# Turning the probabilities of an attention layer by DMA instead of on TensorE

## The chip, the cores and the metric

The kernel runs on one core of a Trainium2 chip. Times are microseconds (us) of device time of one execution of the whole program.

## The reference

A two-layer streaming encoder, one inference step. There are 2048 prompt tokens (one sequence) and 64 sample tokens with caches of earlier keys and values; the model width is 1024. Both layers do

```python
q, k, v, gate = project(x, norm_g, w_in, q_g, k_g, n_heads, n_kv)   # RMS norm, one projection, RMS norm of q and k by head
o = attend(q, k, v, bias, valid, sinks)                              # softmax(q k / 8 + bias) v in a band of chunks of 64
y = x + (o * silu(gate)) @ w_out
```

Layer A has 16 query heads and 2 key heads, a band of the own chunk and 2 before it, and sinks. Layer B has 16 heads of 64 with keys and values of their own, a band of the own chunk and 8 before it, and a learned bias by clipped distance. For a tile of 128 query tokens of layer B the band is 640 keys wide, five blocks of 128. The results are the new activations of prompt and sample and the rolled key and value caches.

## The kernel before

The program is one long stream for TensorE, written out by hand in order; the other engines are ordered by a scheduler, which follows the order of the program text where it sees no reason against it. All DMAs are issued from the queue of SP (`load` and `store` are both `nc.sync.dma_start`), which works strictly in order: an instruction that waits holds up all behind it.

Two things are interleaved on TensorE. The `Filler` runs through jobs of projections (input projections of the layer, then the output projection), and the attention of the layer runs beside it: `pipeline()` in `layer_b` emits a piece of attention, calls `filler.to(mark)` to put in projection matmuls up to a mark, emits the next piece, and so on. Small work of the other engines (norms of q and k, splits of weights, copies) waits in a `Background` queue and is handed out by budget (`bg.share`).

Precision comes from splitting: a number is kept as a high and a low half, and a product is the sum of two or three matmuls. In layer B the weights (`wh`, `wl`), the activations (`xx`), the values (`VH`, both halves side by side in 128 columns) and the probabilities (`ph`, `pl`) are f16 halves; q and k are fp32r halves.

Layer B works by head pair (8 of them) and unit (8 units of 256 prompt tokens, two tiles each, and one unit of 64 sample tokens). A prompt unit has four steps, one for each tile `i` and head `h`, in the order (0,0), (1,0), (0,1), (1,1). One step:

- `scores(it, i, h)`: matmuls of q (L1354) and of its low half (L1355) against the band's keys into a PSUM buffer "sb"; DVE adds the bias and takes the minimum (L1358); ACT takes the exponential of up to 640 columns and its sum (L1362). `p` now holds the probabilities with queries on partitions, in a buffer of three.
- filler matmuls, half a step of them;
- `values` of the step before: up to five turns on TensorE (`transpose`, a helper, so all have line L799) bring `p` into another "sb" buffer with keys on partitions; ACT copies it to the high half `ph`, scaled (L774), DVE computes the low half `pl` (L775);
- `products` of a head, when both of its tiles are done: 12 matmuls of values against `ph` and `pl` (L1449). The short ones, for blocks that only one tile has, stand between the turns of `values`; the others follow.
- filler matmuls, the other half of the step.

After the second head, `finish_pairs` adds the halves, multiplies by the gate and stores to `ogb` (L1196 to L1200), from where the output projection loads it.

The queries and keys of the next unit are prepared in `queries`, after the second step of a unit. It copies the high half of q to the other partitions by two DMAs (L1301). Activations are loaded again for each head pair from a DRAM copy (`xsb`), one chunk of 256 KB in each of `XN = 7` buffers (L501); raw weights go through `WB = 3` buffers (L430). A new head pair's weights are prepared under the running one's units; `scan` loads of later weights measure their range.

Of the kernel before, what the change touches and what calls it, by code (L numbers as in the profile page):

```python
# [19 lines left out]
KC = 8  # L20
# [30 lines left out]
HB, WB_, PB, VB = 2.0 ** 10, 2.0 ** 14, 2.0 ** 14, 16.0  # L51

@with_exitstack
def hybrid_encoder_kernel(
# [152 lines left out]
    def input_across(h):  # L207
        across(h, h + 1)
        e, r, o = row[:, 16:17], row[:, 17:18], row[:, 20:23]
        powers(row[:, h : h + 1], e, r)  # L210
        times(o[:, 0:1], r, WB_)
        times(o[:, 1:2], e, 1 / (HB * WB_))
        times(o[:, 2:3], e, 0.5 / (VB * PB))
# [197 lines left out]
    def load_weights(g, *specs, scale=None):  # L411
# [75 lines left out]
    def load_act(  # L487
# [9 lines left out]

        if cached:
# [14 lines left out]
        def split(c):  # L513
            def fn():
# [3 lines left out]
                xx = t("xx", [P, 4 * OT], XN, dt)  # L518
# [19 lines left out]
                if cache is not None:  # L538
                    store(kept(c), wide(xx[:, : 4 * T]))
                if not squares:  # L540
                    fetch()
# [227 lines left out]
    def split_to(dst_hi, dst_lo, src, scale=None):  # L769
# [8 lines left out]
        return a, b  # L778

# [411 lines left out]
    def finish_pairs(Ov, gtv, n, dst):  # L1191
# [8 lines left out]
        store(dst, o1v)  # L1200


    def layer_b():
# [4 lines left out]
        def add_unit(hp, unit):  # L1208
# [21 lines left out]
            def gen():  # L1230
# [3 lines left out]
                if "VH" not in held:  # L1234
                    held["VH"] = t("values", [P, NT, 2, P], 1, F16)
# [37 lines left out]
        def queries(it):  # L1273
# [25 lines left out]
            if it not in its[-2:]:  # L1299
# [21 lines left out]
        def scores(it, i, h):  # L1321
# [5 lines left out]
            if i == 0 and h == 0:  # L1327
# [5 lines left out]
                it.base = 0 if u == NU else max(tt - 4, 0)  # L1333
# [23 lines left out]
            for r, b, c in soft:  # L1357
# [3 lines left out]
                )  # L1361
            ex = nc.scalar.activation(  # L1362
# [3 lines left out]
            bg.anchor(mi, ex)  # L1366
            if c == w - 1:
# [15 lines left out]
        def values(it, i, h, short):  # L1383
            u, T, tiles = it.unit
            tt, t0, n = tiles[i]
            if i == 0:
                it.ph[h], it.pl[h] = (
                    t(x, [P, 5, 256], 2, F32R if u == NU else F16) for x in ("ph", "pl")
                )
            if u == NU:  # L1390
                n, m, kb = P, 3, 0
            else:
                kt0 = max(tt - 4, 0)
                m, kb = tt - kt0 + 1, kt0 - it.base
            PT = psum_b("sb", 1024, 2)
            PTv = PT.rearrange("p (c x) -> p c x", x=P)
            for c in range(m):
                transpose(PTv[:, (kb + c) % 5, :n], it.p[i, h][:n, c * P : (c + 1) * P])
                if short:
                    short.pop(0)()  # L1400
            while short:
                short.pop(0)()
            bg.anchor(*split_to(
                it.ph[h][:, :m, t0 : t0 + n], it.pl[h][:, :m, t0 : t0 + n], PTv[:, :m, :n],
                None if u == NU else PB,
            ))

        def then(it, i, h):
            if it.unit[0] == NU:
                return [([], lambda: sample_outputs(it)), ([], lambda: sample_turned(it))]  # L1410
            if i == len(it.unit[2]) - 1:
                return [products(it, h)]
            return []
# [23 lines left out]
        def products(it, h):  # L1437
            u, T, tiles = it.unit
            ta, tb = tiles[0][0], tiles[1][0]
            VH = held["VH"]  # L1440
            full = [(VH[:, kt, h], kt - it.base, 0, UT) for kt in range(max(tb - 4, 0), ta + 1)]
            short = [(VH[:, ta - 4, h], ta - 4 - it.base, 0, P)] if ta >= 4 else []
            short.append((VH[:, tb, h], (tb - it.base) % 5, P, UT))
            last = len(full) - 1

            def product(x, low, start=False, stop=False):
                vt, c, q0, q1_ = x
                p = (it.ph, it.pl)[low][h]
                nc.tensor.matmul(it.O[:, h * T + q0 : h * T + q1_], vt, p[:, c, q0:q1_], start=start, stop=stop)  # L1449
# [312 lines left out]
```

## Time and profile before

| | us |
|---|---|
| median of 3 runs | 2256.91 |
| lowest and highest | 2255.82, 2259.93 |
| the profiled execution | 2247.8 |
| its span, first to last instruction | 2245.8 |

The profile is one execution. Layer A and its output projection take up to about 900 us, the attention of layer B runs from about 950 to 2100 us, and the output projection of layer B ends the program. The rows of a group give the line, the engine, the operation and the tiles, then the busy time and the mean duration of one in nanoseconds, then the time that the engine stood idle just before them and what ended it. A row of the timeline gives start, duration, engine, line and tile. "SPq" is the queue of SP, with the time that it takes to issue a DMA.

### The profile page before, as it was taken

The numbers are of one execution on the slowest core, as the hardware profiler recorded it, in microseconds if no ns is written. First come the engines' busy times: TensorE is split into PE (matmuls) and PEld (weight loads), VectorE is DVE, ScalarE is ACT, GpSimd is POOL, SyncE is SP. The second block draws the span as 40 slices with busy tenths as digits, with TensorE's granted clock in tenths as the row PEclk, the third lists the DMA queues.
The fourth block names the chain that finished last, engine by engine and source line by source line (L and its number), as shares of the span: only waits on it lengthen the run. The fifth ranks groups of instructions, "written<-read, shape, count | busy, mean of one in ns | idle before, by whom it ended". The sixth has DMA issues, their size and how long they took to land.

```text
span 2245.8 us, 42218 instructions
## 1 busy us (share of the span) xinstructions
PE 2175.2 (97%) x13931; PEld 1650.5 (73%) x13931; DVE 1565.0 (70%) x4042; ACT 1422.5 (63%) x3610; POOL 858.9 (38%) x1396
## 2 busy tenths in 40 slices
PE   7999999999999998989999999999999999999999
PEld 6888888888889996556666666666666666567888
DVE  6769777677675556777777776777777777677543
ACT  6878777777784333676666666766666667566421
POOL 5645544343454455753333233332333333232000
PEclk9999999999999999999999999999999999999999
DMA  8856547856446666444243333443443424233664
GB/s 272 281 166 218 179 138 223 240 176 193 162 139 193 222 192 213 149 134 138 87 151 112 117 119 108 131 122 96 123 124 108 133 87 133 82 92 121 186 201 156
DMA packets 274811, 349.00 MB, mean 155 GB/s; under 512 B 32080, under 2 KB 195680, under 8 KB 274560
## 3 DMA queue, kind: packets, MB, share of 16 engines
q1 hardware_dynamic: 274592, 346.30, 50.0%
q8 instruction: 110, 1.80, 0.3%
q14 instruction: 109, 0.89, 0.1%
HBM read 257.59 MB, written 73.43 MB: 147 GB/s over the span
## 4 chain that ended last, share of the span: by engine, by line
PE 37%; DVE 9%; ACT 6%; DMA 4%; issue 3%; POOL 1%; SPq 0%; ACTq 0%; DVEq 0%; POOLq 0%
PE pj L640 6%; PE pj L642 6%; PE pj L641 6%; PE sb L799 4%; PE o L1449 3%; DVE pl L775 2%; PE pj L1605 2%; PE pj L1607 2%; PE pj L1606 2%; DMA scan<-in_w_in_b_dram 2%; ACT p L1362 2%; DVE p L1358 2%; PE sb L1354 2%; PE sb L1355 2%; DMA scan<-in_w_o_b_dram 1%
## 5 line engine op out<-in xcount | busy, mean ns | idle before, releaser
L640 PE MATMUL pj<-wh,xx 128*128 128x512 f16 (+2 forms) x1648 | 639.9, 388 | 2.9 <-ACT pb L663 1.5
L641 PE MATMUL pj<-wl,xx 128*128 128x512 f16 (+2 forms) x1648 | 624.6, 379 | 5.5 <-DVE wl L451 5.5
L642 PE MATMUL pj<-wh,xx 128*128 128x512 f16 (+2 forms) x1648 | 624.7, 379 | 1.3 <-POOL xx L530 1.3
L1362 ACT ACTIVATE p<-p,nm 128x640 f32<-128x640 f32 (+5 forms) x264 | 199.4, 755 | 238.4 <-DVE nm L1358 236.0
L1605 PE MATMUL pj<-xx,wh 128*128 128x264 f32 (+1 forms) x1024 | 289.5, 283 | 3.0 <-DVE res L1615 1.3
L1607 PE MATMUL pj<-xx,wl 128*128 128x264 f32 (+1 forms) x1024 | 286.4, 280 | 1.7 <-DVE wl L441 1.1
L1606 PE MATMUL pj<-xx,wh 128*128 128x264 f32 (+1 forms) x1024 | 287.0, 280 | 0.0
L775 DVE SCALAR_TENSOR_TENSOR pl<-sb,ph 128x640 f16<-128x640 f32 (+4 forms) x256 | 188.9, 738 | 107.4 <-ACT ph L774 104.6
L799 PE MATMUL sb<-ident,p 128*128 128x128 f32 x1144 | 205.9, 277 | 14.2 <-DVE pl L775 12.6
L530 POOL TENSOR_TENSOR xx<-xraw,xx 128x528 fp32r<-128x528 f32 (+4 forms) x144 | 182.7, 1288 | 93.6 <-ACT xx L529 84.2
L1199 POOL TENSOR_TENSOR o<-gt,o 128x256 f32<-128x256 f32 (+1 forms) x132 | 100.0, 757 | 309.4 <-ACT p L1107 89.4
L1358 DVE CUSTOM_DVE_ANT_0 p<-sb,BT 128x640 f32<-128x640 f32 (+5 forms) x272 | 196.2, 721 | 26.3 <-PE sb L1355 22.0
L799 PEld LDWEIGHTS sb<-ident,p 128*128 128x128 f32 x1144 | 148.2, 141 | 72.0 <-DVE pl L775 25.1
L722 POOL TENSOR_TENSOR f<-f,mhalf 128x4 f32<-128x4 f32 (+2 forms) x187 | 192.8, 1031 | 14.4
L717 POOL TENSOR_TENSOR sq<-pa 128x256 f32<-128x256 f32 (+2 forms) x187 | 113.3, 606 | 214.3 <-ACT pa L676 145.9
L642 PEld LDWEIGHTS <-xx 128*128 128x128 f16 x1024 | 100.7, 98 | 126.5 <-issue 5.2
L774 ACT ACTIVATE ph<-sb 128x640 f16<-128x640 f32 (+4 forms) x256 | 160.4, 627 | 50.7 <-PE sb L799 49.3
L1107 ACT ACTIVATE p<-p,nm 128x257 f32<-128x257 f32 (+2 forms) x272 | 134.3, 497 | 45.5 <-DVE nm L1101 40.5
L640 PEld LDWEIGHTS <-xx 128*128 128x128 f16 x1024 | 100.4, 98 | 78.4 <-issue 2.2
L641 PEld LDWEIGHTS <-xx 128*128 128x128 f16 x1024 | 101.1, 99 | 67.5 <-issue 2.1
L1449 PE MATMUL o<-pl,values 128*128 128x256 f16 (+1 forms) x672 | 148.9, 255 | 0.0
L1449 PEld LDWEIGHTS <-values 128*128 128x128 f16 x1344 | 133.3, 100 | 16.0
(255 smaller groups left out, 5100.1 us busy)
## 6 DMA issues: line engine op xcount, KB each, us to landing
xx<-xsb SPq DMA_DIRECT2D x224, 256.0 KB, 2.8
xx<-xsa SPq DMA_DIRECT2D x88, 512.0 KB, 4.8
xraw<-oga SPq DMA_DIRECT2D x64, 264.0 KB, 3.6
xraw<-ogb SPq DMA_DIRECT2D x64, 264.0 KB, 3.3
xsa<-xx SPq DMA_DIRECT2D x32, 512.0 KB, 4.1
scan<-in_w_in_b_dram SPq DMA_DIRECT2D x64, 256.0 KB, 3.5
wraw<-in_w_in_b_dram SPq DMA_DIRECT2D x64, 256.0 KB, 3.3
q<-q SPq DMA_DIRECT2D x250, 64.0 KB, 2.3
```

The source lines that it names most:

```text
L640: nc.tensor.matmul(ps[:n, :C], xh, wh, start=k == 0, stop=False)
L641: nc.tensor.matmul(ps[:n, :C], xh, wl, start=False, stop=False)
L642: nc.tensor.matmul(ps[:n, :C], xl, wh, start=False, stop=k == KC - 1)
L722: nc.gpsimd.tensor_tensor(fv, fv, mhalf[:n, :H], op=ALU.pow)
L775: b = nc.vector.scalar_tensor_tensor(dst_lo, src, scale, wide(dst_hi), op0=ALU.mult, op1=ALU.subtract)
L799: nc.tensor.transpose(out, in_, ident[:n, :n])
L1358: mi = nc.vector.tensor_tensor_reduce(out=p[r, :nk], in0=S[r, o : o + nk], in1=b, op0=ALU.add, op1=ALU.min, scale=1.0, scalar=3e38, accum_ ...
L1362: ex = nc.scalar.activation(p[:n, :nk], p[:n, :nk], AF.Exp, scale=-1.0, bias=it.nm[:n, c : c + 1], accum_out=it.sm[:n, c : c + 1],)
L1449: nc.tensor.matmul(it.O[:, h * T + q0 : h * T + q1_], vt, p[:, c, q0:q1_], start=start, stop=stop)
L1605: nc.tensor.matmul(ps[:, :OT], wh, oh, start=k == 0, stop=False)
L1606: nc.tensor.matmul(ps[:, :OT], wh, ol, start=False, stop=False)
L1607: nc.tensor.matmul(ps[:, :OT], wl, oh, start=False, stop=k == KC - 1)
```

## The change

Layer B no longer turns its prompt probabilities on TensorE. After the exponential, ACT copies `p` to f16 (the high half) and GpSimd subtracts it from `p` (the low half), both into one of three buffers `two`, half and half by block, cut out of memory that the values do not use. The factor 2^14 that the scaled copy had applied is put into the exponent (an addition of its logarithm on DVE ahead of the exponential). One step later `turn_p` issues a transposing DMA that turns all blocks and halves of the step, up to 128 x 1280 f16, into `ph` (first head) or `pl` (second head). The products of a head follow three steps (`LAG`) after the scores of its second tile, in one burst; `moving` picks the block, for both tiles at once by a strided access where both have it. The sample unit keeps its turns on TensorE.

Beside that: two activation chunks share a buffer slot of layer B, so that its loads and the stores of the cached copy move two chunks at once; scaled raw weights go into the twelve buffers "wl", and both halves of a weight block into one "wh" buffer; and the stores of outputs, keys and values and the copies of q are kept in a list `held["later"]` and issued at the next `flush()`, half a step later. The turn of the gate uses an "sb" buffer in place of "tp".

```diff
+LAG = 3
+HALF = 5 * 2 * P
@@ fetch and split of load_weights
-                if spare and c % 2 and c > WB:
+                if scale is not None:
+                    raw = t("wl", [P, 512], WN)
+                elif spare and c % 2 and c > WB:
...
-                w.h = wh = t("wh", [P, J, C], WN, dt)
-                w.l = wl = t("wl", [P, J, C], WN, dt)
+                if scale is None:
+                    wh, wl = (t(x, [P, J, C], WN, dt) for x in ("wh", "wl"))
+                else:
+                    both = t("wh", [P, 2, C], WN, dt)
+                    wh, wl = both[:, 0:1], both[:, 1:2]
+                w.h, w.l = wh, wl
@@ load_act
+        if cached and dt == F16:
+            for c in (0, 2):
+                xx = t("xx", [P, 8 * OT], XN, dt)
+                held["last"] = load(
+                    xx[:, : 8 * T], cache[:, o * 2 * KC + 4 * c * T : o * 2 * KC + 4 * (c + 2) * T]
+                ).ins
+                x.parts += [parts_of(xx[:, 4 * T * e : 4 * T * (e + 1)], T, joint) for e in range(2)]
+            return x
@@ store_kv
-            store(kdst, ko[rows])
-            store(vdst, v)
+            if layer:
+                held["later"].append(lambda: (store(kdst, ko[rows]), store(vdst, v)))
...
@@ queries
+            def copies():
                 for hh, rows in enumerate(halves):
                     load(q1[hh][halves[1 - hh]].bitcast(F32), q1[hh][rows].bitcast(F32))
+
+            if it not in its[-2:]:
+                held["later"].append(copies)
@@ scores
+            if u != NU:
+                nc.vector.tensor_scalar(
+                    it.nm[:, c : c + 1], it.nm[:, c : c + 1], math.log(PB), 1.0,
+                    op0=ALU.add, op1=ALU.mult,
+                )
             ex = nc.scalar.activation(
...
+            if u != NU:
+                parts(it, i, h, p, nk // P)
...
+        def parts(it, i, h, p, m):
+            held["turn"] = r = (held["turn"] + 1) % 3
+            it.two = it.two if i or h else {}
+            it.two[i, h] = two = held["two"][:, 5 * r : 5 * r + m]
+            pv = p.rearrange("p (c q) -> p c q", q=P)[:, :m]
+            hi = nc.scalar.copy(two[:, :, 0, :], pv)
+            lo = nc.gpsimd.tensor_tensor(two[:, :, 1, :], pv, two[:, :, 0, :], op=ALU.subtract)
+            bg.anchor(hi, lo)
+
+        def turn_p(it, i, h):
+            if i == 0:
+                it.ph[h] = t(("ph", "pl")[h], [P, 2 * HALF], 2, F16)
+            two = it.two[i, h].rearrange("p c l q -> p (c l q)")
+            m = two.shape[1]
+            nc.sync.dma_start_transpose(
+                it.ph[h][:, HALF * i : HALF * i + m].rearrange("p (c q) -> p c q", q=P), two
+            )
...
+            todo = [(1, lambda: turn_p(it, i, h))]
             if i == len(it.unit[2]) - 1:
-                return [products(it, h)]
-            return []
+                todo.append((LAG, lambda: products(it, h)))
+            return todo
@@ products
+            for kt in [kb] + [k for k in range(ka, tb + 1) if k != kb]:
+                for low in range(2):
+                    x, q0, q1_ = moving(kt, low)
+                    nc.tensor.matmul(
+                        it.O[:, h * T + q0 : h * T + q1_], held["VH"][:, kt, h], x,
+                        start=kt == kb and not low, stop=kt == tb and low == 1,
+                    )
...
+        def flush():
+            later, held["later"] = held["later"], []
+            for fn in later:
+                fn()
@@ pipeline, in each step
+            def due(at):
+                flush()
+                now = [fn for d, fn in todo if d <= at]
+                todo[:] = [(d, fn) for d, fn in todo if d > at]
+                for fn in now:
+                    fn()
...
                     scores(it, i, h)
                     bg.share(BL, BP_, KC)
                     goal(2 * y + 1)
-                    short, nxt = todo.pop(0) if todo else ([], None)
-                    if prev is not None:
-                        values(*prev, short)
-                        bg.share(BL, BP_, KC)
-                        todo += then(*prev)
...
+                    due(step)
+                    bg.share(BL, BP_, KC)
+                    todo += [(step + d, fn) for d, fn in then(it, i, h)]
+                    step += 1
```

More of the change, by code (lines that the diff above doesn't have):

```diff
@@ L1199, in finish_pairs @@
         nc.gpsimd.tensor_tensor(o1v, gtv, o1v, op=ALU.mult)
-        store(dst, o1v)
+        if later:
+            held["later"].append(lambda: store(dst, o1v))
+        else:
+            store(dst, o1v)
     def layer_b():
@@ L1396, in values @@
             PTv = PT.rearrange("p (c x) -> p c x", x=P)
[L1397 to L1406, printed above, removed]
+            for c in range(3):
+                transpose(PTv[:, c, :], it.p[0, 0][:, c * P : (c + 1) * P])
@@ L1439, in products @@
             ta, tb = tiles[0][0], tiles[1][0]
[L1440 to L1449, printed above, removed]
@@ L1525, in pipeline @@
                 assert x + 2 >= len(its) or its[x + 2].ready
[L1526 to L1527 removed]
             while todo:
                 filler.to(filler.done + 2.6)
[L1530 to L1533 removed]
+                due(step)
+                step += 1
+            due(step)
         return pipeline
```

121 lines of the change are left out of this document (65 added, 56 removed).

## The prediction

> **What bounds the kernel now.** I read the page's head first, then the windows of layer B, then the groups by line, and last the timeline of one unit, engine by engine.
>
> ```profile
> span 2245.8 us, 42218 instructions
> PE 2175.2 (97%) x13931; PEld 1650.5 (73%) x13931; DVE 1565.0 (70%) x4042; ACT 1422.5 (63%) x3610; POOL 858.9 (38%) x1396
> 1200.00:1400.00 200.00, 197.42 (x1230) 129.44 (x1228) 145.70 (x374) 127.54 (x332) 65.00 (x119) 1.00 0.38 113
> L799 PE MATMUL sb<-ident,p 128*128 128x128 f32 x1144 | 205.9, 277 | 14.2 <-DVE pl L775 12.6
> ```
>
> PE (TensorE) bounds it: it is busy for 97% of the span and for 197.4 of 200 us in the middle of layer B, at full clock, while in the same stretch DVE has 145.7, ACT 127.5, POOL 65.0 and the DMA engines a share of 0.38 at 113 GB/s. The group that the change attacks is the last row: PE turns the probabilities block by block, 1144 times. Of these, 3 in each of 8 head pairs belong to the sample unit and stay, so 1120 go. But the 205.9 us are not what their removal is worth: matmuls overlap, and what counts is how far apart they start.
>
> ```profile
> 1402.66 0.28 PE L799 MATMUL sb<-ident,p 128*128 128x128 f32 x1
> 1402.77 0.22 PE L1449 MATMUL o<-pl,values 128*128 128x128 f16 x1
> 1402.83 0.28 PE L799 MATMUL sb<-ident,p 128*128 128x128 f32 x1
> 1408.84 0.71 PE L799 MATMUL sb<-ident,p 128*128 128x128 f32 x5
> 1409.38 0.38 PE L640 MATMUL pj<-wh,xx 128*128 128x512 f16 x1
> 1415.34 0.52 PE L1354 MATMUL sb<-KA,q 128*128 128x384 f32 x1
> 1432.71 0.53 PE L1354 MATMUL sb<-KA,q 128*128 128x384 f32 x1
> ```
>
> Five turns start at 1408.84 and the next projection matmul at 1409.38: 0.54 us, 0.108 us each. Where a product stands between two turns, the turn is again 0.11 us of the 0.17 (1402.66 to 1402.77). The last two rows are the first scores of two consecutive units (two token tiles, two heads, so four steps): 17.37 us per unit, 4.34 per step. The 1120 turns make 56 full units of 20.
>
> **What goes from PE.** 1120 turns at 0.109 us: -122.1 us. With them goes the wait for the PSUM buffer in which they land (12.6 us, the releaser "DVE pl L775" of the row above). The products stay: as many matmuls on the same columns, only gathered in one burst, since their place between turns hid nothing (a short product costs its 0.06 us there too). A full unit becomes 17.37 - 20 x 0.109 = 15.2 us, a step 3.8.
>
> **What the other engines get.** All of it must fit in 15.2 us per unit; 200 us of the window hold 11.5 units.
>
> ```profile
> L774 ACT ACTIVATE ph<-sb 128x640 f16<-128x640 f32 x192 | 133.0, 693 | 37.7 <-PE sb L799 36.8
> L775 DVE SCALAR_TENSOR_TENSOR pl<-sb,ph 128x640 f16<-128x640 f32 x192 | 157.7, 822 | 87.1 <-ACT ph L774 84.8
> L1358 DVE DVE_READ_ACCUMULATOR2_ANT nm<- 128x1 f32 x256 | 21.1, 82 | 0.0
> L530 POOL TENSOR_TENSOR xx<-xraw,xx 128x528 fp32r<-128x528 f32 x64 | 88.3, 1408 | 63.8 <-ACT xx L529 57.1 <-issue 6.6
> L530 POOL TENSOR_TENSOR xx<-xraw,xx 128x512 f16<-128x512 f32 x32 | 37.9, 1203 | 8.7 <-ACT xx L529 6.1 <-DMA xraw<-x 2.6
> L529 ACT CAST xx<-xraw 128x528 fp32r<-128x528 f32 x64 | 39.6, 633 | 31.3 <-PE pj L1607 28.4
> ```
>
> ACT: the high half was a scaled copy out of PSUM (0.69 us), and is now a copy out of SBUF; by the 128x528 cast, 0.633 x 640/528 = 0.77. ACT goes from 127.5/11.5 = 11.1 to 11.4 us. DVE loses 0.82 and gets a 128x1 addition (about the 0.08 of the accumulator read) per step: 12.7 to 9.7. POOL gets the subtraction that DVE had: 1.203 x 640/512 = 1.50 by the nearer row (f16 out), 1.408 x 640/528 = 1.71 by the other; I take 1.6, so 5.65 + 6.4 = 12.1 of 15.2. POOL is the next engine, at 79%, but under PE. To pass PE the subtraction would have to take 2.4 us.
>
> **The transfers.** 256 transposing DMAs of 128x1280 f16 (327,680 bytes in a full step) are new, 144 plain ones go (activation chunks in pairs). No row shows a transposing transfer. What rows show:
>
> ```profile
> q<-q SPq DMA_DIRECT2D x250, 64.0 KB, 2.3
> xx<-xsb SPq DMA_DIRECT2D x224, 256.0 KB, 2.8
> 1417.77 0.38 SPq L501 DMA_DIRECT2D xx<-xsb  x1
> 1407.09 0.32 SPq L1200 DMA_DIRECT2D ogb<-o  x1
> 1434.93 0.42 SPq L783 DMA_DIRECT2D res<-in_ckt_b_dram  x1
> ```
>
> An issue holds SP's queue for 0.32 to 0.42 us whatever its size, and 256 KB land after 2.8. The lower bound of a transpose is that: 0.38 us of the queue, 3.0 to landing. The upper bound takes it as ten transfers of one 128x128 block each: 3.8 us of the queue. (Landing one pair of blocks after another like the 64 KB row would be 5 x 2.3 = 11.5 us; that is a rival below.) In the built program 9.65 plain issues stand beside each four transposes, 3.7 us. So SP holds 5.2 us per unit at the lower bound and 18.9 at the upper; the transposes must stay under (15.2 - 3.7)/4 = 2.9 us of the queue not to bound the kernel, and at 3.4 the gain is gone. I take the lower half, since each is one instruction and the nearest rows do not grow with size. Data: 4 x 327,680 bytes at 113/0.38 = 297 GB/s are 4.4 us beside the 6.6 there are: 11.0 of 15.2.
>
> The Trainium skill (DMA: Bandwidth & Descriptors, Latency and other measured facts) gives 261 GB/s for a transposing DMA with a strided middle dimension; an estimate from it is 5.0 us in place of 4.4, and the sum is the same. No trace here shows it.
>
> **Is three steps enough?** The path from a score to its product, by one step of the trace:
>
> ```profile
> 1400.30 0.53 PE L1354 MATMUL sb<-KA,q 128*128 128x384 f32 x1
> 1401.72 0.82 DVE L1358 CUSTOM_DVE_ANT_0 p<-sb,BT 128x640 f32<-128x640 f32 x1
> 1402.58 0.83 ACT L1362 ACTIVATE p<-p,nm 128x640 f32<-128x640 f32 x1 [1.97 <-DVE nm L1358]
> 1403.32 0.19 ACT L1362 ACTIVATION_READ_ACCUMULATOR p<-p,nm 128x1 f32 x1
> ```
>
> Exp is done 3.2 us after the score starts. Then the addition 0.1, the copy 0.8, the subtraction 1.6, and up to one foreign POOL instruction ahead, about 0.8: 6.5. The transfer lands at about 9.5, or at 13.3 with the upper queue price. The product stands three steps and half of one later: 3.5 x 3.8 = 13.3. So at the lower price there are 3.8 us of slack, and DVE, ACT and POOL, 64 to 79% busy, eat some. Only the second tile of each head has three steps, so 128 products can wait; I put one in four late by 1 us: +32 us (from 0 to +75). The same slack covers the buffer that the copy and subtraction write (three in turn, so ACT waits for the transfer of three steps before).
>
> **What else moves.** Stores of the outputs and of k and v and the q copies go out half a step later. Behind a transpose that waits for POOL, everything on SP waits: the loads are a unit ahead, the q copies have 1.5 steps (5.7 us) for 2.3 of landing, stores only hold buffers that are needed a unit later. Zero each; the q copies cost what a transpose is late by beyond 3.4 us. Fewer, larger activation loads and deeper weight buffers end queue waits that delay nobody on PE:
>
> ```profile
> SPq L501 <- PE pj L642: 319.8, 132, 11.3
> PE sb L799 <- DVE pl L775: 11.1, 16, 1.5
> ```
>
> These are the longest waits of the queue and of PE from 1000 to 2000 us; PE has no wait for an xx load there. So zero, but these queue waits (up to 11.3 us) would have held the transposes back, and must be gone for the three steps to hold.
>
> **Sum.** Against the profiled execution of 2247.8 us: 2247.8 - 122.1 - 12.6 + 32 = 2145. The median of the runs is 2256.9, 9.1 more: 2154.
>
> **Rivals.** *The queue bounds it* (slower): the transpose is issued block by block, 0.38 us each, 3.8 in all. A unit takes 4 x 3.8 + 3.7 = 18.9, 1.5 more than now, times 56: 2343; at 0.405 a block 2400, at 0.32 2208; it decides from 0.34 a block. For it: ten blocks are ten times what a plain issue describes, and SP already stands blocked for long. Against: every plain row is flat in size. Chance 0.20, of which 0.16 slower.
>
> *Blocks land one after the other* (slower): each pair of blocks costs the 2.3 us of a 64 KB transfer, 11.5 us per transpose, 46 us per unit against 17.4: +28.6 x 56, about 3860. Against: 256 KB land in 2.8 us, so parts do overlap in plain transfers. Chance 0.08.
>
> The Trainium skill (VectorE: DVE Perf Modes, The three transpose paths) speaks for this one: it gives 390 ns for a 128x128 turn on TensorE and 1309 ns by DMA, and advises TensorE where PSUM will do; an estimate of ten blocks in a row from it is 13.1 us. The trace has PE at 0.108 us a turn in a stream, and no DMA row to set beside the other.
>
> *The chain is late* (no change): the path takes 15.2 us instead of 9.5 to 11, through queues on ACT, POOL and SP; then a step lasts 15.2/3.5 = 4.34 us as now: 2257. For it: ACT, POOL and DMA each wait in turn, and waits on ACT for DVE reach 3.4 us. Chance 0.14: 0.06 faster, 0.03 same, 0.05 slower.
>
> *More than the stream*: if the removed 202 us of busy time (1120 of 1144) go in full, 80 more: 2075. The start times speak against. Chance 0.05.
>
> **Numbers.** Forecast 0.53, with its own range 2120 (no product waits) to 2200 (75 us of them). Within 0.2% (4.5 us) is what this measurement cannot tell from no change. Faster: 0.53 + 0.05 + 0.06 + 0.04 (the first rival's low end) = 0.68; same 0.03; slower 0.16 + 0.08 + 0.05 = 0.29. The range runs from 2075 (the last rival) to 2400 (the first at 0.405 a block): it leaves out the serial landing, 0.08, the first rival's tail, 0.06, and 0.04 beyond its ends elsewhere, under 0.2.
>
> **What would show it.** Right: PE over 95% busy from 1000 us on, units of 15.2 us, the products' wait for DMA under 75 us in total, transposes under 2.9 us on SP's queue and about 3 to landing, POOL near 12 us per unit. Wrong: SP issuing without a gap and products waiting for DMA in each unit (first rival), a landing above 10 us (second), units of 17 us with ACT waiting for DMA at the new copy (third).

## The result: 1% slower, and the profile after

The changed kernel takes 2280.22 us (median of four runs, 2276.87 to 2283.43), the kernel before 2256.45: a ratio of 1.0099, 95% interval 1.007 to 1.0128. The forecast was 2154. The profiled execution took 2276.87 us.

The head of the page after, the group that took the subtraction over, and the page's list of DMA issues (KB each, median us to landing):

```profile
span 2275.0 us, 40902 instructions
PE 2099.6 (92%) x12811; PEld 1545.2 (68%) x12811; DVE 1516.5 (67%) x4042; ACT 1439.3 (63%) x3610; POOL 1184.2 (52%) x1652
L1440 POOL TENSOR_TENSOR values<-p,values 128x640 f16<-128x640 f32 (+4 forms) x256 | 326.1, 1275 | 344.5 <-ACT values L1439 323.6
ph<-values SPq DMA_TRANSPOSE x128, 3.7
pl<-values SPq DMA_TRANSPOSE x128, 3.6
q<-q SPq DMA_DIRECT2D x250, 64.0 KB, 3.1
```

The turns are gone: PE's busy time fell by 75.6 us and the span grew by 29.2. So PE (TensorE) now stands still for longer. The windows show where: three stretches of layer B (the first head pair, the second, the rest), first the kernel before, then the one after. The columns are PE, PEld, DVE, ACT and POOL, each with its busy time and instructions, then the granted clock, the DMA share and GB/s.

```profile
895.00:1060.00 165.00, 155.62 (x957) 100.55 (x955) 123.52 (x297) 108.66 (x276) 89.04 (x127) 1.00 0.44 138
1060.00:1200.00 140.00, 137.57 (x850) 90.00 (x849) 103.69 (x258) 91.19 (x231) 44.43 (x81) 1.00 0.40 123
1200.00:2060.00 860.00, 840.22 (x5253) 555.27 (x5251) 630.49 (x1569) 558.83 (x1414) 277.15 (x497) 1.00 0.37 113
```

```profile
895.00:1060.00 165.00, 120.51 (x621) 70.91 (x618) 92.44 (x234) 88.78 (x213) 108.43 (x129) 0.86 0.66 174
1060.00:1200.00 140.00, 128.91 (x724) 77.79 (x723) 95.91 (x260) 92.82 (x232) 83.94 (x114) 0.96 0.77 171
1200.00:2060.00 860.00, 784.67 (x4443) 476.11 (x4443) 601.25 (x1585) 572.41 (x1426) 520.64 (x698) 0.97 0.75 175
```

Three things stand there. PE falls from 98% to 91% in the long stretch and from 94% to 73% in the first head pair. The granted clock is no longer 1.00. And the DMA share doubled in the long stretch. The waits of PE from 890 to 2135 us (us in total, times, longest), first before, then after:

```profile
PE sb L799 <- DVE pl L775: 12.6, 18, 1.5
PE tp L799 <- DVE pa L735: 4.6, 1, 4.6
```

```profile
PE tp L833 <- DVE pa L763: 41.4, 11, 9.0
PE o L1516 <- DMA pl<-values: 29.0, 11, 4.5
PE o L1474 <- DVE o L1234: 21.4, 8, 3.1
PE sb L1398 <- DMA q<-q: 14.1, 10, 2.7
PE tp L833 <- DVE scl L202: 8.9, 5, 1.8
```

The wait for the PSUM buffer of the turns is gone. The products wait for their transposes (second row of after), but that is under a third of the idle time that came in. The largest wait is an old one grown ninefold: PE waits to turn q and k (tp L833) until DVE has normed them (pa L763).

The clock is the other half. Ten-microsecond windows of the first head pair after:

```profile
930.00:940.00 10.00, 5.08 (x20) 3.07 (x21) 3.42 (x9) 3.47 (x10) 5.67 (x7) 0.53 0.86 248
940.00:950.00 10.00, 10.00 (x59) 6.22 (x57) 6.04 (x18) 6.17 (x14) 5.87 (x9) 1.00 0.28 61
950.00:960.00 10.00, 1.97 (x11) 0.87 (x8) 1.32 (x7) 3.48 (x8) 9.48 (x10) 0.82 0.62 151
960.00:970.00 10.00, 9.92 (x50) 6.50 (x51) 6.20 (x15) 4.74 (x12) 3.34 (x5) 0.84 0.60 181
```

PE stands idle for 8 us between 950 and 960, and in the next window, where it is busy all the time, it gets 0.84 of its clock and starts 50 matmuls, against 59 from 940 to 950 at full clock. In the trace's clock records from 890 to 2135 us the clock is either full or half, half for pieces of 3.4 us or a multiple: 3 such pieces before, 27 after. In the 3.4 us ahead of each of the 27, PE had been idle for at least 1.74 us.

From the first score of layer B to the first score of its last prompt unit, the time therefore divides into idle time of PE (gaps over 0.1 us between its matmuls), time lost at half clock (half of each such piece), and the rest, PE's **stream** (the time that falls under both counted once). In the profiled executions:

| us | stretch | idle | half clock | stream |
|---|---|---|---|---|
| before | 1174.2 | 33.7 | 3.4 | 1137.3 |
| after | 1201.2 | 135.5 | 59.7 | 1017.1 |

The stream shrank by 120.2 us; 101.8 of idle time and 45.4 at half clock (counted once) came in. The first head pair alone went from 157.1 to 198.7 us, more than the whole loss; the next six changed by between -3.9 and +1.4, where 17 us less were forecast for each (eight units of 2.2).

### The profile page after: what moved, and what is told of

Read it like the earlier page. It is cut to its first block, busy times and chain, and to the rows that moved or that the text cites. A ratio compares the mean times of both kernels' runs of the same rounds, so it can differ in the third digit from the quotient of the medians.

```text
span 2275.0 us, 40902 instructions
## 1 busy us (share of the span) xinstructions
PE 2099.6 (92%) x12811; PEld 1545.2 (68%) x12811; DVE 1516.5 (67%) x4042; ACT 1439.3 (63%) x3610; POOL 1184.2 (52%) x1652
## 5 line engine op out<-in xcount | busy, mean ns | idle before, releaser
L668 PE MATMUL pj<-wh,xx 128*128 128x512 f16 (+2 forms) x1648 | 651.9, 396 | 4.5 <-ACT pb L691 3.0
L670 PE MATMUL pj<-wh,xx 128*128 128x512 f16 (+2 forms) x1648 | 634.2, 385 | 5.9 <-POOL xx L553 5.9
L1440 POOL TENSOR_TENSOR values<-p,values 128x640 f16<-128x640 f32 (+4 forms) x256 | 326.1, 1275 | 344.5 <-ACT values L1439 323.6
L669 PE MATMUL pj<-wh,xx 128*128 128x512 f16 x1024 | 399.8, 390 | 0.0
L669 PE MATMUL pj<-wl,xx 128*128 128x512 f32 (+1 forms) x624 | 234.6, 376 | 2.0 <-DVE wl L459 2.0
L763 DVE TENSOR_TENSOR pa<-pa,f 128x256 f32<-128x256 f32 (+3 forms) x221 | 140.8, 637 | 90.7 <-POOL f L750 85.7
L750 POOL TENSOR_TENSOR f<-f,mhalf 128x4 f32<-128x4 f32 (+2 forms) x187 | 187.4, 1002 | 11.4
L1516 PEld LDWEIGHTS <-values 128*128 128x128 f16 x1344 | 125.7, 100 | 76.8 <-issue 24.4
L1439 ACT CAST values<-p 128x640 f16<-128x640 f32 (+4 forms) x256 | 168.1, 657 | 6.6 <-DMA pl<-values 0.7
L772 DVE SCALAR_TENSOR_TENSOR pb<-sq,pb 128x128 f32<-128x128 f32 (+3 forms) x204 | 121.6, 598 | 67.4 <-ACT sq L771 66.0
L745 POOL TENSOR_TENSOR sq<-pa 128x256 f32<-128x256 f32 (+2 forms) x187 | 126.0, 675 | 39.0 <-ACT pa L691 28.1
L1669 PE MATMUL pj<-xx,wl 128*128 128x264 f32 x512 | 145.0, 283 | 0.7 <-DVE wl L452 0.7
```

Source lines behind the costliest of these rows:

```text
L668: nc.tensor.matmul(ps[:n, :C], xh, wh, start=k == 0, stop=False)
L669: nc.tensor.matmul(ps[:n, :C], xh, wl, start=False, stop=False)
L670: nc.tensor.matmul(ps[:n, :C], xl, wh, start=False, stop=k == KC - 1)
L750: nc.gpsimd.tensor_tensor(fv, fv, mhalf[:n, :H], op=ALU.pow)
L1439: hi = nc.scalar.copy(two[:, :, 0, :], pv)
L1440: lo = nc.gpsimd.tensor_tensor(two[:, :, 1, :], pv, two[:, :, 0, :], op=ALU.subtract)
```

## Experiments

The runs were made on several chips. Each ratio is to the kernel before on the run's own chip (2251 to 2264 us), and kernels are compared by their ratios, 1% being 22.6 us. The kernel before differs by 0.5% between the chips, so a difference between runs of two chips is less sure than the intervals say; where the plain times tell another size, both are given. Lines are those of the changed kernel.

### Is it the turning, or the rest of the change?

`e7_rest_only` is the kernel before with the change's buffers (two chunks a slot, "wl", "wh") and late stores, without `parts` and `turn_p`: the turns stay on TensorE.

> The kernel before with all of the change but the turning: two activation chunks per slot, deep weight buffers, stores and q copies half a step late; TensorE turns the probabilities as before. All theories of the turning: within 5 us of the kernel before (2254.6), since no wait of TensorE there hangs on those. If the late q copies or the buffers cost by themselves: 2262 or more, and the loss of the change is in part theirs.

2248.53 us, ratio 0.996 (0.9945 to 0.9974). The rest of the change gains 0.4%. All the loss is in the turning: 1.0099 against 0.996, 31 us.

### Single waits, one at a time

`e1_no_add` leaves the addition of L1407 out, and with it the factor 2^14.

```diff
-            if u != NU:
-                nc.vector.tensor_scalar(
-                    it.nm[:, c : c + 1], it.nm[:, c : c + 1], math.log(PB), 1.0,
-                    op0=ALU.add, op1=ALU.mult,
-                )
```

> The addition of the logarithm ahead of the exponential is left out, and with it the factor 2^14, so that the f16 halves of small probabilities are coarser; nothing else changes. Stall theory (TensorE's stream is as short as forecast, and single stalls at a few places eat it): only the stalls of the last products on their transpose get shorter, up to 29 us of waits and half as much of clock, so 5 to 30 us off 2280. Chain theory (the path from score to product is too long in every step, since the addition waits on DVE behind other work, 0.5 us and up to 2.5): 40 us or more off. If neither matters to TensorE: 2280 as it is.

2259.19, ratio 1.0019 (1.0005 to 1.0034): some 18 us, for an operation that computes nothing to speak of. One step of the timeline after shows how it can cost that much:

```profile
1488.05 0.82 DVE L1402 CUSTOM_DVE_ANT_0 p<-sb,BT 128x640 f32<-128x640 f32 x1
1488.80 0.08 DVE L1402 DVE_READ_ACCUMULATOR2_ANT nm<- 128x1 f32 x1
1488.80 0.82 DVE L459 SCALAR_TENSOR_TENSOR wh<-wl,gsb,wh 128x512 f16<-128x512 f32 x1
1489.55 0.41 DVE L746 TENSOR_REDUCE f<-sq 128x4 f32<-128x256 f32 x1
1489.87 0.74 DVE L459 SCALAR_TENSOR_TENSOR wh<-wl,gsb,wh 128x512 f16<-128x512 f32 x1
1490.53 0.14 DVE L1407 TENSOR_SCALAR nm<-nm 128x1 f32<-128x1 f32 x1
1490.77 0.83 ACT L1411 ACTIVATE p<-p,nm 128x640 f32<-128x640 f32 x1 [2.60 <-DVE nm L1407]
```

It takes 0.14 us, but comes 1.65 us after the minimum that it adds to, behind three other operations of VectorE; the exponential waits for it. This step is one of the worst: over all 256 the addition comes 0.47 us after the minimum on the mean, and in half of them within 0.13. That the 18 us come from this alone is not shown.

`e2_dve_first_pair` gives the subtraction to VectorE in the first head pair, where GpSimd is fullest.

```diff
-            lo = nc.gpsimd.tensor_tensor(two[:, :, 1, :], pv, two[:, :, 0, :], op=ALU.subtract)
+            eng = nc.vector if it.hp == 0 else nc.gpsimd
+            lo = eng.tensor_tensor(two[:, :, 1, :], pv, two[:, :, 0, :], op=ALU.subtract)
```

> In the first head pair alone the low half is subtracted on DVE in place of GpSimd. Stall theory: the seven waits of the turns of q and k for their norm there (38 us of the 43.7, GpSimd overfull with the splits of the activations) go, and with them the half clock after each, about 20 us: 2220 to 2240. Chain or DMA theory: GpSimd is not what delays the first pair, and the time stays within 10 us of 2280.

2265.85, ratio 1.0039 (1.002 to 1.0058), 14 us, between what the two theories gave. The first head pair falls from 198.7 to 185.5 us, far from its 157.1.

`e3_sample_psum` puts the sample unit's output, which waited at L1474 for the PSUM buffer "o" that late products still held, into "tp"; `e4_lag4` does that and lets the products stand four steps behind.

```diff
-LAG = 3
+LAG = 4
-            O = psum("o", 512, 1)
+            O = psum("tp", 512, 1)
```

> The sample unit's output goes to the PSUM buffer tp instead of o, which the products of the prompt unit before still hold. Stall theory: eight waits of 2 to 3 us (21.4 in all) and eight stretches of half clock (14) go: 2245 to 2260. If the stall only moves to the next instruction that needs the same data: 2275 to 2285.

> Products four steps behind their scores instead of three, and the sample output in tp as in the third kernel (with o the program cannot run). Stall theory: beyond the third kernel, the products' waits for the transposes (45 us with those of the weight loads) and their half clock go: 2200 to 2220. Chain theory: the same or more. If the transposes are late because the queue cannot keep up, a step more buys nothing lasting: as the third kernel.

e3: 2280.57 (1.0111, 1.0082 to 1.014); the wait at L1474 is gone and 20.4 us have come up at the turns, which now wait for the same buffer "tp". e4: 2269.72 (1.0066, 1.0049 to 1.0083). Its waits of PE from 890 to 2135 us:

```profile
PE tp L833 <- DVE pa L763: 38.8, 8, 8.8
PE sb L1398 <- DMA q<-q: 14.8, 8, 2.8
PE o L833 <- ACT gt L1222: 12.2, 4, 3.5
PE o L1516 <- DMA pl<-values: 0.4, 1, 0.4
```

The products wait for nothing any more (29.0 us to 0.4), yet the idle time of the stretch only falls from 135.5 to 132.6. So three steps were too few for the chain, but a fourth is worth no more than 10 us, far from the 2200 to 2220 of the theory.

### The same cures together

`e9_all_cures` has all four (addition out, subtraction on VectorE in the first pair, four steps, "tp"); `e10_all_now` issues the copies of q at once besides (`copies()` for `held["later"].append(copies)`).

> Four small cures at once on the changed kernel: the addition and its 2^14 left out, the low half subtracted on VectorE in the first head pair alone, products four steps behind instead of three, the sample unit's output in the PSUM buffer of the turns. One at a time they gave 21, 14 and 10 us (the last two together). Theory (the losses are separate stalls, each with its own cause): they add, 2280 - 45 = 2235 us, below the kernel before (2256), idle time of TensorE in layer B near 137 - 7 - 10 - 4 = 116 us. Rival (VectorE, ScalarE and GpSimd are short of time, and a stall that is cured shows at the next wait): no more than the best of them gives, 2255 to 2262 us.

> The four cures, and the copies of the queries into the other half issued at once, as the kernel before does, instead of half a step later. Theory (late copies cost): the waits for q<-q at the scores (12.5 us in seven waits with four steps of lag) go, 8 to 15 us less than with the four cures alone. Rival (the copies land late because the queue's engines are shared with the transposes, not for their place): within 4 us of it, the waits staying.

2268.31 (1.0085, 1.0058 to 1.0111) and 2271.85 (1.0084, 1.0064 to 1.0105). Together the cures give 3 us by the ratios and 12 by the times (13 in the profiled stretch), no more than e1 or e2 alone, where 45 were to be added up: the rival holds in kind, though 2268 lies 6 us above its range. Idle time falls to 124.8 us, and the half-clock loss rises to 64.9. No wait of a product for a transpose is left above 0.3 us. Issuing the copies of q at once gains nothing, and 11.7 of their 13.5 us of waits stay, as the rival of e10 has it. So single waits do not explain the loss; something makes many of them late.

### The subtraction

`e5_no_low` leaves it out: the low half is zeros, turned and multiplied as before. `e8_dve_low` moves it to VectorE everywhere (without the addition), `e11_split` in the second head and the first pair (with the four cures).

```diff
-            lo = nc.gpsimd.tensor_tensor(two[:, :, 1, :], pv, two[:, :, 0, :], op=ALU.subtract)
```

> GpSimd's subtraction is left out; the low halves are set to zero once, so the products run as before but with the high half of the probabilities alone. The first four kernels showed that a stall taken away comes back elsewhere, with the idle time of TensorE in layer B near 130 us in each. GpSimd theory (the subtraction, 326 us of it, delays the norms behind it on GpSimd and, by the shared access, DVE): idle time falls to 50 us or less, 2170 to 2200. DMA theory (the transposes and what stands behind them on the queue are late): only the chain gets 1.6 us shorter, 2255 to 2275. Queue and GpSimd both at their limit: between, 2205 to 2250.

> The low half is computed on DVE in place of GpSimd in all head pairs, and the addition of the logarithm is left out (with the factor 2^14, so small probabilities are coarser). DVE gets back the 0.8 us per step that it had before, GpSimd is as free as before. GpSimd theory: idle time of TensorE under 80 us, 2200 to 2235. DMA theory: 2250 to 2265, as without the addition alone (2259).

> The four cures, and the low half of the second head subtracted on VectorE in every head pair, that of the first head on GpSimd. Theory (GpSimd's subtraction, alone and by slowing VectorE's operations beside it, holds the chain): GpSimd falls from 128 to about 95 us of 200, VectorE keeps near 145, 15 to 30 us less than with the four cures alone. Rival (any engine that takes the subtraction is too full with it): within 8 us of it, as the subtraction on VectorE everywhere gave nothing (2284 against 2259 without the addition).

e5: 2210.79, ratio 0.9803 (0.9781 to 0.9826), 67 us less than with it, and the first head pair is back at 163.1 us. That lies between the two theories, in the range set for queue and GpSimd both at their limit. e8: 2284.15 (1.013, 1.0112 to 1.0149), above both of its theories. e11: 2278.64 (1.0121, 1.0102 to 1.014), without the gain of its theory. So the subtraction costs its tens of microseconds on whichever engine does it; with the cures it is 58 (`e12_no_low_all` below against e9, 0.9829 against 1.0085). Since in e9 no products wait for transposes, and ScalarE waits only 5.0 us for the buffers that are turned, neither the chain's length nor the buffers explain the price; what is left is the load. One path of it is in the groups of VectorE, here by shape: the gate (pb) and the norm of q and k (pa) before, after, with the low half out, and with it on VectorE.

```profile
L744 DVE SCALAR_TENSOR_TENSOR pb<-sq,pb 128x128 f32<-128x128 f32 x128 | 39.7, 314 | 7.9 <-ACT sq L743 6.6
L735 DVE TENSOR_TENSOR pa<-pa,f 128x256 f32<-128x256 f32 x192 | 98.6, 514 | 32.7 <-POOL f L722 31.2 <-POOL f L730 0.5
```

```profile
L772 DVE SCALAR_TENSOR_TENSOR pb<-sq,pb 128x128 f32<-128x128 f32 x128 | 76.3, 599 | 51.7 <-ACT sq L771 51.1
L763 DVE TENSOR_TENSOR pa<-pa,f 128x256 f32<-128x256 f32 x192 | 127.5, 664 | 83.4 <-POOL f L750 81.7 <-POOL f L758 0.5
```

```profile
L772 DVE SCALAR_TENSOR_TENSOR pb<-sq,pb 128x128 f32<-128x128 f32 x128 | 40.2, 315 | 12.7 <-ACT sq L771 11.8
L763 DVE TENSOR_TENSOR pa<-pa,f 128x256 f32<-128x256 f32 x192 | 100.1, 521 | 53.4 <-POOL f L750 51.1 <-POOL f L758 0.5
```

```profile
L772 DVE SCALAR_TENSOR_TENSOR pb<-sq,pb 128x128 f32<-128x128 f32 x128 | 43.4, 343 | 1.6 <-ACT sq L771 0.8
L1435 DVE TENSOR_TENSOR values<-p,values 128x640 f16<-128x640 f32 (+4 forms) x256 | 204.3, 800 | 120.1 <-ACT values L1434 118.0 <-DMA ogb<-o 0.6
```

The gate of 128x128 takes 314 ns on the mean, 599 when GpSimd does the subtractions, and 315 and 343 when it doesn't: the same instruction is nearly twice as long. The norm is longer too, and waits for GpSimd's powers (f L750) for 81.7 us instead of 31.2. That norm is in the chain that PE waits for at L833: squares on GpSimd, sums on VectorE, powers on GpSimd, scaling on VectorE, turns on PE. On VectorE the subtraction takes 204.3 us instead, somewhat more than the 188.9 that the split L775 had taken, and the chain waits behind it.

The single instructions show what makes the gate longer. Of the 128 after, 21 start while GpSimd is idle, and these take 273 to 293 ns. 56 start while a subtraction runs, and nine in ten of them end 145 to 152 ns after that subtraction ends, whenever they began:

```profile
1281.26 1.40 POOL L1440 TENSOR_TENSOR values<-p,values 128x640 f16<-128x640 f32 x1 [2.19 <-ACT values L1439]
1281.43 1.38 DVE L772 SCALAR_TENSOR_TENSOR pb<-sq,pb 128x128 f32<-128x128 f32 x1 [2.01 <-ACT sq L771]
```

The subtraction ends at 1282.66 and the gate at 1282.81. So the gate waits for the subtraction's end, though it uses none of its data.

The Trainium skill (SBUF — State Buffer, SBUF: two separate sides) says that VectorE, when an operation has two inputs in SBUF, and GpSimd share a pair of ports that one of them holds for a whole instruction while the other waits. The trace agrees, by these 56 ends. How much of the 67 us these waits make, and how much the fuller engines alone, is not told apart; e8 has few of them at the gate, and its load costs as much.

### The transfers

`e6_one_block` turns one pair of blocks by each DMA, which all products read; `e17_no_low_one_block` does it with the low half out, beside `e12_no_low_all` (e5 with the addition out, four steps and "tp").

```diff
-            m = two.shape[1]
+            m = 2 * P
+            two = two[:, :m]
```

> Each transposing DMA turns one block of keys, both halves, in place of up to five, and all products read that block; the copy, the subtraction and all waits between the engines stay. DMA theory: issue and landing shrink (1.3 to about 0.6 us and 3.7 to about 2.5), data falls by four fifths; 2190 to 2220. GpSimd theory: 2265 to 2280, as the stalls of the norms do not hang on the transfers.

> The low half left out (zeros in its place, turned and multiplied as before), with the addition out, four steps of lag and the sample unit's output in the buffer of the turns: the turning by DMA without the subtraction's load. Theory (what stays with the low half out, 92 us idle and 29 us of clock, is lateness and the one PSUM buffer of the outputs): 2211 falls to 2150 to 2180 us. Rival (the transposes themselves, by their share of the DMA engines, hold the rest): 2200 to 2211 us.

> As the kernel with the low half left out (zeros), no addition, four steps of lag: but each transposing DMA turns one pair of blocks instead of up to five, and all products read that pair, so the values are wrong in all but one block and the transfers of the turning are a fifth. Theory (the transfers of the turning make the copies of the queries and the data late: q<-q 26 us of waits): 2213 falls to 2180 to 2195 us. Rival (they cost nothing, as with the subtraction in: 2272 against 2280): 2205 to 2213 us.

e6: 2272.41, ratio 1.0077 (1.0057 to 1.0097), no clear gain although the DMA share of the long stretch falls from 0.75 to 0.47; the gate of 128x128 takes 618 ns there, so its length does not come from the transfers. e12: 2213.55 (0.9829, 0.9808 to 0.985): the cures give nothing with the low half out either. e17: 2184.98 (0.9656, 0.9639 to 0.9674), 39 us less than e12 by the ratios, 29 by the times. The waits for the copies of q from 890 to 2135 us, in e12 and in e17:

```profile
PE sb L1399 <- DMA q<-q: 26.0, 11, 4.5
```

```profile
PE sb L1399 <- DMA q<-q: 3.5, 4, 1.9
```

So four fifths of the transfers cost nothing clear while the subtraction was in, and 1.3 to 1.7% once it was out. `e16_exp_turned` leaves the copy on ScalarE out as well, the exponential writing its f16 into the buffer that is turned.

> As the kernel with the low half left out (zeros), no addition, four steps of lag: but the exponential writes its f16 straight into the buffer that is turned, so the copy on ScalarE (168 us in all) is left out too, and the chain is shorter by it. Theory (the extra work on the other engines holds the time): 2213 falls by 20 to 50 us, ScalarE from 135 to about 105 of 200 us. Rival (the transfers hold it): 2205 to 2213 us.

2207.31, ratio 0.9755 (0.9738 to 0.9771): 17 us less than e12 by the ratios and 6 by the times, for 168 us of ScalarE's time. That is less than its theory gave, and by the time within its rival's range.

### Is TensorE still the bound?

`e13_turns_too` puts as many turns of a constant on TensorE, beside the DMA turning; `e14_no_low_turns` does it to e12.

```diff
             if h == 0:
                 it.O = psum("o", 512, 1)
+            for _ in range(ta - ka + 1 + tb - kb + 1):
+                transpose(it.O[:, h * T : h * T + P], ident)
```

> The changed kernel with as many turns of a constant on TensorE, ahead of each group of products, as the kernel before has of the probabilities (1120 in all, 122 us by the forecast's pitch), on top of the turning by DMA. Their output is written over by the products. Theory (the other engines set the pace, TensorE fills the gaps): the turns go into idle time, 2280 to 2310 us, and idle time of TensorE in layer B falls from 137 us to below 70. Rival (the stalls are separate waits that happen whatever TensorE does beside them): 2280 + 122 = 2400 us, idle time as it was.

> The same turns of a constant on TensorE, put on the kernel with the low half left out (zeros in its place), no addition, four steps of lag and the sample unit's output in the buffer of the turns (2213 us). Theory (without the subtraction TensorE sets the pace again, and what idle time it has is fixed waits): 2213 + 122 = 2335 us less the clock's share, above 2300. Rival (the other engines set the pace here too): 2230 to 2260 us, near the kernel before, which does the same products and turns.

2359.37 (1.0423, 1.0404 to 1.0442) and 2304.04 (1.0182, 1.0154 to 1.0209): 73 and 80 us for a stream that grows by 118 and 114 (table below). Neither theory of e13 fits; e14 lies just above the 2300 of its theory, 31 us short of the 2335. About two thirds of the turns show, one third goes into time that PE had idle or at half clock. TensorE still sets most of the pace, and by these two runs a microsecond taken from it is worth about two thirds of one.

### With one half in place of two

Both large prices hang on the split of each probability in two f16. `e18_one_half_dma` has the DMA turning with one f16 per probability, `e19_one_half_pe` the turning on TensorE.

> The turning by DMA with one f16 per probability instead of two: the exponential writes it straight into the buffer that is turned, half as many blocks are turned, and the products of the low half (672 of them, 74.5 us of TensorE) are left out; no addition, four steps of lag, the sample unit's output in the buffer of the turns. Theory (price of the transfers falls by half, the products' time is given back for two thirds, as the turns' was): 2207 - 20 - 50 = 2137 us. Rival (TensorE has stopped setting the pace): 2180 to 2207 us.

> One f16 per probability with the turns kept on TensorE: the kernel with only the buffers and the late stores of the change, one copy by ScalarE out of PSUM instead of the split by ScalarE and VectorE (189 us of VectorE left out), and no products of the low half (74.5 us of TensorE). Theory (TensorE is its bound, 30 us idle): 2249 - 75 = 2174 us, so that the turning by DMA wins by some 37 us when no low half is wanted. Rival (the turning by DMA costs as much as it frees even then): e18 and e19 within 10 us of each other.

2140.92, ratio 0.9473 (0.9452 to 0.9494), and 2191.6, ratio 0.9709 (0.9684 to 0.9734). With nothing to subtract and half as much to turn, the DMA turning is ahead by 51 us. Both are faster than either kernel, but they drop half the bits of a probability that the kernels keep; of those that keep them, e7 is the fastest.

The layer B stretch of the kernels that carry the argument, divided as above:

| us | stretch | idle | half clock | stream |
|---|---|---|---|---|
| e7, rest of the change only | 1172.2 | 30.5 | 5.1 | 1137.0 |
| after | 1201.2 | 135.5 | 59.7 | 1017.1 |
| e9, four cures | 1187.9 | 124.8 | 64.9 | 1012.6 |
| e13, after with turns | 1280.6 | 111.9 | 46.1 | 1135.4 |
| e12, low half out | 1134.1 | 93.1 | 29.0 | 1014.8 |
| e14, that with turns | 1212.5 | 65.4 | 20.5 | 1129.1 |
| e17, and a fifth of the transfers | 1102.7 | 71.6 | 20.5 | 1012.9 |
| e18, one half, by DMA | 1062.2 | 81.1 | 30.7 | 955.7 |
| e19, one half, on PE | 1112.1 | 36.1 | 5.2 | 1071.2 |

The stream of the kernels that turn by DMA and do the same products is the same within 5 us; they differ in idle time and half clock.

## Why the prediction was wrong

**What was to be seen.** PE was to be over 95% busy from 1000 us on and is at 91%; units of 15.2 us were to follow and are 16.4 in the median after the first head pair, 25.4 in it. The other signs came as named (products waiting under 75 us, transposes under 2.9 us of the queue, GpSimd at 9.9 us per unit against 12), so none of those could tell that the forecast was failing.

**What goes from PE: right.** -122.1 us were forecast. The stream lost 120.2, and e13, with the turns put back, has the stream of before within 2. The 12.6 us wait for the PSUM buffer went too.

**The transfers: right that they don't bind, and so the first two rivals fall.** The transposes after, by their line (ns on the queue: min/median/max, then the first and the last start):

```profile
L1448 SPq DMA_TRANSPOSE ph<-values x128: 1190/1362/2727, 901.7 to 2108.3; - x128
L1448 SPq DMA_TRANSPOSE pl<-values x128: 1177/1344/3191, 913.8 to 2120.1; - x128
```

A transpose holds SP's queue for 1.34 to 1.36 us, between the bounds 0.38 and 3.8 and under the 2.9 that would have bound the kernel, but 3.6 times the lower bound. It lands after 3.7 us against 3.0. The Trainium skill's 1309 ns per block by DMA (VectorE: DVE Perf Modes, The three transpose paths) would make ten blocks 13.1 us if they went one by one, by the estimate in the prediction; the 3.7 us of ten speak against that reading, and e6 lands one pair after 2.4 to 2.8.

**Is three steps enough: right in size, in part by luck, and beside the point.** +32 us were set for products that wait for transposes, 32 waits of 1 us; 29.0 are in the row, but in 11 waits of up to 4.5 us. And the sum took this for the only new wait. PE's idle time rose by 101.8.

**What the other engines get: the step that failed.** It worked from one window, 1200 to 1400 us, and asked only whether each engine's sum fits under PE's.

- The first head pair was not looked at. There GpSimd also splits activations: 89.0 of 165 us before, 10.6 per unit of 19.6 (157.1/8), where the forecast had 5.65. With 5.1 for the subtraction (four of 1275 ns) it needs 15.7 of the 17.4 us that a unit there would have had. The unit became 24.8 (198.7/8).
- VectorE was to fall from 12.7 to 9.7 us per unit, 168 us in 56 units. It fell by 48.5. The split L775 went (189 us), but the addition took 37.5 against 0.08 x 256 = 20, and three groups that read two SBUF operands grew beside GpSimd: the gate by 46, the norm by 30, the weights' low halves by 19 (all shapes).
- "POOL is the next engine, but under PE" took a fit of sums for a fit of the path. The subtraction itself was cheaper than forecast (1.43 us for 128x640 on the mean against 1.6), and GpSimd is at 61% in the long stretch. Yet leaving it out gains 67 us (e5). The sum had nothing for what it does to others: the norms of q and k, which PE waits for, pass twice through GpSimd and twice through VectorE, and VectorE's operations wait for the end of a running subtraction. The addition, "0.1 us" in the chain, cost some 18 us by e1 alone; with the other cures nothing can be told of it.

**A term that the sum lacked: the clock.** A stall of PE brings on a piece at half clock. 59.7 us were lost so against 3.4, 45.4 more when overlaps are counted once; before had only three such pieces, and the sum priced idle time at its length alone.

**What else moves: right on the half step, not on the copies of q.** Issuing the copies at once gains nothing (e10). But PE waits 14.1 us for them after and not at all before; with the low half out, these waits fall from 26.0 to 3.5 us when the transfers are cut to a fifth (e17). The buffers gained 0.4% (e7), where zero was forecast.

**The data: half right.** The transfers were to hide in the DMA engines' free time, 11.0 of 15.2 us; the share measured is 0.75 against 0.72, but of units of 16.4 us, which makes 12.3 us per unit. And sharing has a price: e17 against e12 puts it at 29 to 39 us with the low half out, and e6 at 5, within its uncertainty, in the kernel as changed.

**The rivals.** "The chain is late" came nearest in time (2257). Its mechanism is not what happened: with a step more for the chain (e4) the products stop waiting and 2270 us stay, and of its sign, ScalarE waiting for DMA at the new copy, there is one wait of 0.7 us. What happened was not among the rivals: the work that left PE lands on two engines through which PE's other inputs pass.

**The balance.** By these runs' ratios: two thirds of 122 us gained, 76 to 86; the low half 67, the transfers 5 to 39, the copy 17 lost. That gives 3 to 47 us more than e7, where 31 are measured. The prices overlap, as e6 and e9 show, so no closer sum is claimed. What makes up the 65.4 us of idle time that e14 keeps against the 30.5 of e7 (nearly the same stream) may be partly those transfers and the copy; it stays open.

## What to carry to other kernels

Before moving work off the bounding engine, follow the other inputs of that engine: if they pass through the engines that take the work over, a load that fits in the sum still makes each of them late, and it must be looked at in the stage where those engines are fullest, not in a typical one. Curing the waits that the profile then names mostly moves them about, as four cures together did here; leaving load out is what helped. And price a stall of TensorE at more than its length, a saved microsecond of it at less than one.

## What the runs showed of the hardware

- The clock of TensorE is full or half, and changes in pieces of 3.4 us: 27 pieces at half clock in layer B after, in 21 cases one of 3.4 us alone, otherwise two or three in a row, against 3 before. Ahead of each of the 27, PE was idle for 1.74 us or more of 3.4; of the other stretches of 3.4 us, counted on from those pieces, none that full clock follows has more than 1.90. The Trainium skill (TensorE: Matmul & The Clock Gate, Part 1) describes such a gate with windows of 3.4 us and two rates, and puts the penalty of the ramp at under 1% of a typical kernel's span. Here the pieces come again and again, and cost 48.5 us, 2.1% of the span, with what falls into idle time left out.
- A transposing DMA of 128x1280 f16 from SBUF to SBUF: 1.34 to 1.36 us of the queue, 3.6 to 3.7 us to landing, and a fifth of it 2.4 to 2.8 us.
- A 128x128 operation of VectorE on two SBUF operands: 314 ns on the mean, 599 ns in the kernel where GpSimd subtracts two SBUF operands. Where it starts during a subtraction, it ends some 0.15 us after that; the norm of 128x256 0.28 us, the low half of a 128x512 block of weights 0.55 us after.
